# A kernel's last FFN quarter: older blocks first in the down product, two token sums in buffers of their own, a small copy from VectorE to ScalarE

## The chip, the core and the metric

The kernel runs on one core of one Trainium2 chip. The metric is the device time of one execution in microseconds (us). The engines are TensorE (PE; its weight loads are PEld), VectorE (DVE), ScalarE (ACT), GpSimd (POOL) and SyncE (SP), which issues most transfers.

## What is computed

One layer of a hybrid decoder runs over 2,064 prompt tokens (16 learned ones and 2,048) and, beside them, over 8 sampled sequences with one new token each. The mixers (an SSD scan, stick-breaking attention and a gated linear recurrence) come first; the change lies mostly in the feed-forward part behind them:

```python
h = rms_norm(x, p['norm2'])
g, u = jnp.split(jnp.einsum('bld,df->blf', h, p['w_up']), 2, axis=-1)      # 1024 -> 2 * 2816
g, ffn_buf = causal_dwconv(g, ffn_buf, p['ffn_conv_w'], p['ffn_conv_b'])   # 3 taps along the tokens
x = x + jnp.einsum('blf,fd->bld', jax.nn.silu(g) * u, p['w_down'])         # 2816 -> 1024
```

The convolution's last inputs are returned as new state, for the prompt and for each sampled sequence.

## The kernel before

All products keep float32's accuracy by splitting each operand into a rounded part and a rest (`hi`, `lo`; `wh`, `wl`) and by adding three products, so each pair of 128x128 blocks costs three matmuls.

The tokens are cut in four quarters c = 0 to 3. The last has 528 tokens and the 8 sampled ones, 536 columns, worked on as two pieces A and B of 268. The hidden width of 2,816 is 22 blocks f of 128. For the last quarter `ffn(3)` (its plan is `ffn_plan(3)`) does blocks 0 and 1 by plain products (`up`) and then five groups of four, which begin with f = 2, 6, 10, 14 and 18.

- `token_sums` (L1393 to L1409) prepares four differences t[0] to t[3] of the input's columns for each k of 0 to 3: POOL subtracts (L1406), ACT rounds to the first half `tt`, DVE takes the rest (L1409). All four results of a k lie in the ring `pg` of three buffers.
- `seven` (L1411 on) takes two blocks at once, i = 0 for the gate and i = 1 for the up part, in seven products instead of eight, with three PSUM banks. A product is 12 matmuls of 268 columns (L1423). The sums between them, on DVE (L1427), release a bank for the next product: u = banks[1] + p1 releases the bank of the product with tt[3] (called the tt30 product here), and the first use of u and banks[2] releases the one for the last product.
- `conv` adds the taps on DVE (L496, L501 for the sampled tokens), copies the prompt's state on ACT (L498) and the sampled state on DVE (L503); `gate` follows on ACT, DVE and POOL (L1387 to L1390).
- `finish` multiplies gate and up part (L1456, DVE), rounds on ACT (L168) and takes the rest on DVE (L1458): two halves of an act, of which a group needs four.
- `down` (L1488 on) multiplies a group's four acts with W_down, a quarter of the output's rows at a time: four banks of 24 matmuls (L1499), each added to the residual on DVE (L1501). A group's first down quarter is written after the gate part of the next group's first `seven`; by then two acts, the newer pair, have hardly left `finish`.

A scheduler with a simulated timeline sets the order of the instructions within each engine; the streams (main, attention, SSD, samples) are mixed by `mingle`. So an edit in one place can move instructions in others. PSUM banks are handed out in a ring of eight (`mps`).

Of the kernel before, what the change touches and what calls it, by code (L numbers as in the profile page):

```python
# [27 lines left out]
SCOL = CH + TAIL  # L28
# [11 lines left out]
def build(tc, a, o):  # L40
    nc = tc.nc
    ctx = ExitStack()
    with ctx:
# [70 lines left out]
        def pg():  # L114
            return mk(P["ph"], [128, 384], F32, "pg", N["pg"])
# [363 lines left out]
        def conv(outs, c, wts, j, hs, taps, samp, nsamp, rb=None, buf=None):  # L479

            W = ntok(c)
            nt = CH if c < 3 else CH + TAIL
            nh = taps - 1
            buf = tmp() if buf is None else buf
            acc = tmp()
            nc.scalar.copy(buf[:, 0:nh], hs[:, j, :])
            for p, c0, n in outs:
                evac(buf[:, nh + c0:nh + c0 + n], p[:, :n], None if rb is None else rb[:, c0:c0 + n])
                if rb is None:
                    nc.scalar.activation(acc[:, c0:c0 + n], p[:, :n], AF.Identity,  # L490
                                         bias=wts[:, j, taps:taps + 1], scale=wts[:, j, taps - 1:taps])
            if rb is not None:
                nc.scalar.activation(acc[:, :W], buf[:, nh:nh + W], AF.Identity,
                                     bias=wts[:, j, taps:taps + 1], scale=wts[:, j, taps - 1:taps])
            for q in range(nh):
                nc.vector.scalar_tensor_tensor(acc[:, :nt], buf[:, q:q + nt], wts[:, j, q:q + 1], acc[:, :nt],  # L496
                                               ALU.mult, ALU.add)
            nc.scalar.copy(hs[:, j, :], buf[:, nt:nt + nh])  # L498
            if c == 3:
                for q in range(nh):  # L500
                    nc.vector.scalar_tensor_tensor(acc[:, SCOL:SCOL + 8], samp[:, j, q, :], wts[:, j, q:q + 1],  # L501
                                                   acc[:, SCOL:SCOL + 8], ALU.mult, ALU.add)
                nc.vector.tensor_copy(nsamp[:, j, :], buf[:, nh + SCOL:nh + SCOL + 8])  # L503
            return acc


# [873 lines left out]
        def ffn(c):  # L1380
# [12 lines left out]
            def token_sums():  # L1393

                for n in range(4):
                    st["tt", n] = [mk(P["lp"], [128, 4, HW_], F32R, f"tt{n}{j}", 1) for j in range(2)]
                A, B = slice(0, HW_), slice(HW_, W)
                for k in range(4):
                    x = [tmp() for _ in range(2)]
                    for j in range(2):  # L1400
                        nc.scalar.activation(x[j][:, :W], xs[k + 4 * j][:, :W], AF.Copy, scale=g2[:, k + 4 * j:k + 4 * j + 1])
                    t = []
                    for n in range(4):
                        t.append(pg()[:, :HW_])
                        p, q = ((x[0][:, B], x[0][:, A]), (x[1][:, B], t[0]), (x[1][:, B], x[0][:, B]), (x[1][:, A], t[min(n, 1)]))[n]
                        nc.gpsimd.tensor_tensor(t[n], p, q, ALU.subtract)  # L1406
                        hi, lo = [z[:, k, :] for z in st["tt", n]]
                        rounded(hi, t[n])
                        nc.vector.tensor_tensor(lo, t[n], hi.bitcast(F32), ALU.subtract)  # L1409
# [78 lines left out]
            def down(g, i):  # L1488
                wh, wl = wpart()
                nd = NK // len(g)  # L1490
                for d in range(i * nd, (i + 1) * nd):
                    ds_ = slice((d - i * nd) * 128, (d - i * nd) * 128 + 128)
                    for c0, n in pieces(c):
# [302 lines left out]
```

## Time and profile before

| | us |
|---|---|
| median of 3 runs | 2878.35 (2873.82 to 2881.42) |
| the profiled execution | 2877.74 |
| its span in the trace | 2876.1 |
| PE busy in the span | 2740.2 (95%) |
| DVE, ACT, POOL busy | 1955.8, 1314.0, 1230.9 |

All steps below are worked out in the profiled execution. It lies 0.61 us under the median, and 1.6 us of it lie around the span. Times in the trace are counted from the span's start. Matmuls are pipelined, so that the durations of neighbours overlap: what a product costs is read from the start of one to the start of the next.

### The profile page before, as it was taken

What the parts mean: (1) busy time and instruction counts of PE and PEld (TensorE: products, weight loads), DVE (VectorE), ACT (ScalarE), POOL (GpSimd) and SP (SyncE); (2) the same over time, 40 slices, a digit from 0 to 9 for tenths busy, and PEclk for the clock granted to TensorE, in tenths of its full rate; (3) what the DMA queues carried; (4) which work ended last, traced back from release to release, by engine and by line L of the source; (5) the groups of instructions that cost most, each with busy time, mean ns of one, the idle gap of its engine ahead of it and who ended that gap; (6) DMA issues with size and microseconds to landing.
All of it is one profiled execution on the core that took longest, in us unless ns stands there. A gap on an engine that the chain in (4) does not pass through costs nothing. (4 is left out here: it accounts for less than half of the span.)

```text
span 2876.1 us, 44058 instructions
## 1 busy us (share of the span) xinstructions
PE 2740.2 (95%) x14901; PEld 2332.0 (81%) x14901; DVE 1955.8 (68%) x3017; ACT 1314.0 (46%) x2484; POOL 1230.9 (43%) x1597
## 2 busy tenths in 40 slices
PE   8889999899899999899998999999999999999999
PEld 6768778799878877777786788877788888989999
DVE  5673654856758689988674487777677743397775
ACT  4455766776665555445432143434333321433332
POOL 2521211312255554554655455436565530354452
PEclk9999999999999999999999999999999999999999
DMA  9878688668777865878778977675766677566665
GB/s 323 320 270 273 207 265 282 213 214 286 237 256 275 292 223 203 283 256 280 249 234 270 289 249 224 210 251 191 243 229 230 221 231 270 198 208 215 216 210 172
DMA packets 379800, 702.24 MB, mean 244 GB/s; under 512 B 69525, under 2 KB 200262, under 8 KB 379574
## 3 DMA queue, kind: packets, MB, share of 16 engines
q1 hardware_dynamic: 362758, 649.07, 67.3%
q0 software_dynamic: 16384, 50.35, 5.3%
q8 instruction: 118, 1.93, 0.3%
q14 instruction: 108, 0.88, 0.1%
q10 hardware_dynamic: 432, 0.01, 0.0%
HBM read 539.14 MB, written 160.12 MB: 243 GB/s over the span
## 5 line engine op out<-in xcount | busy, mean ns | idle before, releaser
L414 PE MATMUL mm<-hxh,w 128*128 128x512 f32 (+1 forms) x3664 | 1149.9, 387 | 35.7 <-ACT w L168 13.0
L414 PEld LDWEIGHTS mm<-hxh,w 128*128 128x128 f32 x3664 | 677.6, 191 | 173.7 <-ACT w L168 13.4
L414 PE MATMUL mm<-hxl,w 128*128 128x512 f32 (+1 forms) x1832 | 704.5, 385 | 1.2 <-DVE hxl L384 1.0
L414 PEld LDWEIGHTS mm<-hxl,w 128*128 128x128 f32 x1832 | 349.6, 191 | 66.5 <-issue 1.7
L1499 PE MATMUL mm<-ah,w 128*128 128x512 f32 (+1 forms) x968 | 329.6, 387 | 11.9 <-DVE t L1471 4.8
L496 DVE SCALAR_TENSOR_TENSOR t<-t,pack,t 128x512 f32<-128x512 f32 (+1 forms) x284 | 246.3, 867 | 60.8 <-ACT t L490 49.8
L1059 POOL COPY scy<-R 128x1 f32<-128x1 f32 (+1 forms) x245 | 107.2, 438 | 311.2 <-DVE R L1055 283.0
L1055 DVE TENSOR_TENSOR_SCAN R<-R,scy,zcol 128x512 f32<-128x512 f32 (+1 forms) x148 | 204.8, 1385 | 28.6 <-ACT R L1046 28.1
L1499 PEld LDWEIGHTS mm<-ah,w 128*128 128x128 f32 x968 | 182.6, 191 | 49.1 <-DVE x L1501 7.7
L326 POOL TENSOR_TENSOR w<-w,w 128x1024 fp32r<-128x1024 f32 x74 | 185.6, 2508 | 63.3 <-PE mm L414 22.2
L1499 PE MATMUL mm<-al,w 128*128 128x512 f32 (+1 forms) x484 | 185.6, 384 | 2.5 <-DVE al L1473 1.4
L1291 POOL TENSOR_TENSOR pg<-pg,pu 128x384 f32<-128x384 f32 x128 | 137.4, 1082 | 115.1 <-DMA pg<-in_ck 106.9
L1057 DVE TENSOR_TENSOR sz<-sz,R 128x512 f32<-128x512 f32 (+3 forms) x245 | 179.1, 732 | 3.4
L1501 DVE TENSOR_TENSOR x<-x,mm 128x512 f32<-128x512 f32 (+1 forms) x220 | 137.9, 634 | 34.1 <-PE mm L1499 33.7
L1045 ACT ACTIVATE sz<-z,pack 128x512 f32<-128x512 f32 (+3 forms) x180 | 112.2, 623 | 100.5 <-PE z L1128 87.4
L1323 POOL TENSOR_TENSOR pg<-pg,sall 128x384 f32<-128x384 f32 x120 | 115.0, 965 | 97.2 <-DMA pg<-in_cv 96.5
L1292 DVE TENSOR_REDUCE sall<-pg 128x6 f32<-128x384 f32 x128 | 69.8, 547 | 111.1 <-POOL pg L1291 104.0
L1325 DVE TENSOR_TENSOR pu<-pu,pg 128x384 f32<-128x384 f32 x120 | 80.9, 675 | 79.2 <-POOL pg L1323 71.0
L1055 DVE TENSOR_TENSOR_SCAN R<-R,zcol 128x128 f32<-128x128 f32 (+4 forms) x97 | 97.1, 1002 | 49.0 <-POOL R L1134 48.2
L1387 ACT ACTIVATE t<-t 128x512 f32<-128x512 f32 (+1 forms) x88 | 56.2, 639 | 153.8 <-DVE t L496 94.3
L1128 PE MATMUL z<-lk,lq 128*128 128x512 f32 (+3 forms) x360 | 113.0, 387 | 5.2 <-ACT R L1046 5.1
L431 PE MATMUL mm<-w,hxh 128*128 128x390 f32 (+3 forms) x432 | 115.1, 347 | 0.3 <-DMA w<-wsw_v 0.3
(2044 smaller groups left out, 6089.4 us busy)
## 6 DMA issues: line engine op xcount, KB each, us to landing
w<-wsw_up SPq DMA_DIRECT2D x184, 512.0 KB
w<-wsw_down SPq DMA_DIRECT2D x240, 256.0 KB
w<-wsw_inT SPq DMA_DIRECT2D x102, 512.0 KB
wsw_up<-w SPq DMA_DIRECT2D x88, 512.0 KB
w<-wsw_up SPq DMA_DIRECT2D x120, 256.0 KB
w<-wsw_out SPq DMA_DIRECT2D x48, 512.0 KB
pg<-in_ck POOLq DMA_DIRECT2D x128, 192.0 KB, 4.8
pg<-in_cv POOLq DMA_DIRECT2D x128, 192.0 KB, 4.6
```

Source lines behind the costliest of these rows:

```text
L326: (nc.gpsimd if far else nc.vector).tensor_tensor(lo[:, :n], raw[:, :n], hi[:, :n].bitcast(F32), ALU.subtract)
L414: st["pe"] = nc.tensor.matmul(p[:, :n], w_[:, k, :], h_[:, k, c0:c0 + n], start=(i == 0), stop=(i == 3 * NK - 1))
L431: nc.tensor.matmul(pt[i][:r, :n], h_[:, kk, :], w_[:, k, :], start=(kk == 0 and j == 0), stop=(kk == NK - 1 and j == 2))
L496: nc.vector.scalar_tensor_tensor(acc[:, :nt], buf[:, q:q + nt], wts[:, j, q:q + 1], acc[:, :nt], ALU.mult, ALU.add)
L1045: nc.scalar.activation(sz[:rr, :nk], ps[:rr, :nk], AF.Sigmoid, bias=bias)
L1055: nc.vector.tensor_tensor_scan(R[:rr, 0:nk][:, ::-1], R[:rr, 0:nk][:, ::-1], zcol[:rr].to_broadcast([rr, nk]), init, ALU.mult, ALU.add)
L1057: nc.vector.tensor_tensor(sz[:rr, :nk], sz[:rr, :nk], R[:rr, 1:nk + 1], ALU.mult)
L1128: nc.tensor.matmul(p[:, :nk], q[:, t * 128:(t + 1) * 128], kT[:, :nk], start=n == 0, stop=n == 1)
L1291: nc.gpsimd.tensor_tensor(kp, kp, qb[:, :384], ALU.mult)
L1323: nc.gpsimd.tensor_tensor(out.rearrange("p (h d) -> p h d", h=H), vp.rearrange("p (h d) -> p h d", h=H), w6, ALU.mult)
L1499: nc.tensor.matmul(p[:, :n], w_[:, x, ds_], x_[:, s_], start=(x == 0 and j == 0), stop=(x == len(g) - 1 and j == 2))
L1501: nc.vector.tensor_tensor(xs[d][:, s_], xs[d][:, s_], p[:, :n], ALU.add)
```

## The change

There are three edits.

1. In `conv`, the copy of the sampled state goes from DVE to ACT. It runs for the last quarter alone: 22 times for the FFN, 7 for the SSD part, twice for the recurrence.
2. In `token_sums`, t[2] and t[3] of each k share a tile of the pool `a5` (two buffers), and only t[0] and t[1] stay in the ring `pg`.
3. In `down`, the last quarter's first call in each group takes four banks and multiplies the two older acts into all of them (24 matmuls), and then the newer two (24). The residual's four additions follow.

```diff
--- before.py
+++ after.py
@@ -500,7 +500,7 @@
                 for q in range(nh):
                     nc.vector.scalar_tensor_tensor(acc[:, SCOL:SCOL + 8], samp[:, j, q, :], wts[:, j, q:q + 1],
                                                    acc[:, SCOL:SCOL + 8], ALU.mult, ALU.add)
-                nc.vector.tensor_copy(nsamp[:, j, :], buf[:, nh + SCOL:nh + SCOL + 8])
+                nc.scalar.copy(nsamp[:, j, :], buf[:, nh + SCOL:nh + SCOL + 8])
             return acc
 
 
@@ -1400,8 +1400,9 @@
                     for j in range(2):
                         nc.scalar.activation(x[j][:, :W], xs[k + 4 * j][:, :W], AF.Copy, scale=g2[:, k + 4 * j:k + 4 * j + 1])
                     t = []
+                    t23 = mk(P["lp"], [128, WL], F32R, "a5", 2).bitcast(F32)
                     for n in range(4):
-                        t.append(pg()[:, :HW_])
+                        t.append(pg()[:, :HW_] if n < 2 else t23[:, (n - 2) * HW_:(n - 1) * HW_])
                         p, q = ((x[0][:, B], x[0][:, A]), (x[1][:, B], t[0]), (x[1][:, B], x[0][:, B]), (x[1][:, A], t[min(n, 1)]))[n]
                         nc.gpsimd.tensor_tensor(t[n], p, q, ALU.subtract)
                         hi, lo = [z[:, k, :] for z in st["tt", n]]
@@ -1488,6 +1489,20 @@
             def down(g, i):
                 wh, wl = wpart()
                 nd = NK // len(g)
+                if c == 3 and i == 0 and len(g) == 4:
+
+                    cells = [(d, c0, n, mps()) for d in range(nd) for c0, n in pieces(c)]
+                    for xx in ((0, 1), (2, 3)):
+                        for d, c0, n, p in cells:
+                            for x in xx:
+                                hi, lo = acts[g[x]]
+                                for j, (w_, x_) in enumerate(((wh, hi), (wh, lo), (wl, hi))):
+                                    nc.tensor.matmul(p[:, :n], w_[:, x, d * 128:d * 128 + 128], x_[:, c0:c0 + n], start=(x == 0 and j == 0),
+                                                     stop=(x == 3 and j == 2))
+                    for d, c0, n, p in cells:
+                        nc.vector.tensor_tensor(xs[d][:, c0:c0 + n], xs[d][:, c0:c0 + n], p[:, :n], ALU.add)
+                    yield 0.65 * len(g) * nd
+                    return
                 for d in range(i * nd, (i + 1) * nd):
                     ds_ = slice((d - i * nd) * 128, (d - i * nd) * 128 + 128)
                     for c0, n in pieces(c):
```

The scheduler's order moves with it. On PE, in the first down quarter of the group that begins with f = 2, ahead of the tt30 product (ah, al and the first xk pair are the older acts, a5_5418 and a5_5419 the two halves of a newer one; mm, tr, mp and acc are banks). Before:

```order
L1499 MATMUL tr_5452_28484<-a5_5418_28288,w_5437_28377 128x268
L1499 MATMUL mp_5453_28498<-ah_5368_27986,w_5437_28377 128x268
L1499 MATMUL mp_5453_28498<-al_5369_27987,w_5437_28377 128x268
L1499 MATMUL mp_5453_28498<-ah_5368_27986,w_5438_28378 128x268
L1499 MATMUL mp_5453_28498<-xk_5370_27991,w_5437_28377 128x268
L1499 MATMUL mm_5451_28470<-a5_5419_28289,w_5437_28377 128x268
L1499 MATMUL mm_5451_28470<-a5_5418_28288,w_5438_28378 128x268
L1499 MATMUL tr_5452_28484<-a5_5419_28289,w_5437_28377 128x268
L1499 MATMUL tr_5452_28484<-a5_5418_28288,w_5438_28378 128x268
L1499 MATMUL mp_5453_28498<-xk_5371_27992,w_5437_28377 128x268
L1499 MATMUL mp_5453_28498<-xk_5370_27991,w_5438_28378 128x268
L1423 MATMUL mm_5425_28301<-tt30_5251_27217,w_5434_28344 128x268
```

In the changed kernel:

```order
L1500 MATMUL mp_5449_28468<-al_5365_27983,w_5433_28373 128x268
L1500 MATMUL mp_5449_28468<-ah_5364_27982,w_5434_28374 128x268
L1500 MATMUL mp_5449_28468<-xk_5366_27987,w_5433_28373 128x268
L1500 MATMUL mp_5449_28468<-xk_5367_27988,w_5433_28373 128x268
L1500 MATMUL mp_5449_28468<-xk_5366_27987,w_5434_28374 128x268
L1500 MATMUL acc_5450_28469<-ah_5364_27982,w_5433_28373 128x268
L1500 MATMUL acc_5450_28469<-al_5365_27983,w_5433_28373 128x268
L1500 MATMUL acc_5450_28469<-ah_5364_27982,w_5434_28374 128x268
L1500 MATMUL acc_5450_28469<-xk_5366_27987,w_5433_28373 128x268
L1500 MATMUL acc_5450_28469<-xk_5367_27988,w_5433_28373 128x268
L1500 MATMUL acc_5450_28469<-xk_5366_27987,w_5434_28374 128x268
L1424 MATMUL mm_5421_28297<-tt30_5251_27217,w_5430_28340 128x268
```

Ahead of the tt30 product PE now has 24 matmuls with older acts in four banks, where it had 24 in three banks, six of them with the newer act.

On POOL, at the end of the token sums (L1406 before, L1407 in the changed kernel; L301 works on weights, L1390 on the gate). Before:

```order
L1406 TENSOR_TENSOR pg_5270_27275<-t_5266_27260,pg_5268_27267 128x268
L1406 TENSOR_TENSOR pg_5273_27283<-t_5271_27279 128x268
L1406 TENSOR_TENSOR pg_5274_27287<-t_5272_27280,pg_5273_27283 128x268
L301 TENSOR_TENSOR pu_5320_27656<-raw_5284_27369,pu_5308_27565 128x512
L1406 TENSOR_TENSOR pg_5275_27291<-t_5272_27280,t_5271_27279 128x268
L1390 TENSOR_TENSOR t_5282_27354<-t_5282_27354,rb_5240_27198 128x536
L301 TENSOR_TENSOR pu_5352_27859<-raw_5287_27374 128x512
L1406 TENSOR_TENSOR pg_5276_27295<-t_5272_27280,pg_5274_27287 128x268
```

In the changed kernel:

```order
L1407 TENSOR_TENSOR a5_5265_27261<-t_5264_27258,pg_5267_27266 128x268
L1407 TENSOR_TENSOR pg_5271_27281<-t_5268_27276 128x268
L1407 TENSOR_TENSOR a5_5270_27280<-t_5269_27277,t_5268_27276 128x268
L1407 TENSOR_TENSOR pg_5272_27285<-t_5269_27277,pg_5271_27281 128x268
L1407 TENSOR_TENSOR a5_5270_27280<-t_5269_27277,pg_5272_27285 128x268
L301 TENSOR_TENSOR pu_5316_27652<-raw_5280_27365,pu_5304_27561 128x512
L301 TENSOR_TENSOR pu_5348_27855<-raw_5283_27370 128x512
L1390 TENSOR_TENSOR t_5278_27350<-t_5278_27350,rb_5240_27198 128x536
```

The last sum stood behind three operations of other kinds and the one before it behind one; now all sixteen come first.

On DVE, from the last rests of the token sums to the addition that releases the bank acc (L1471 before, L1472 in the changed kernel). Before:

```order
L1409 TENSOR_TENSOR tt31_5252_27218<-pg_5270_27275,tt30_5251_27217 128x268
L1388 TENSOR_TENSOR t_5282_27354<-t_5282_27354,t_5283_27365 128x536
L503 COPY s_ffn_conv1_5244_27209<-t_5295_27486 128x8
L1409 TENSOR_TENSOR tt01_5246_27212<-pg_5273_27283,tt00_5245_27211 128x268
L496 SCALAR_TENSOR_TENSOR t_5296_27487<-t_5295_27486,pack_71_181,t_5296_27487 128x528
L501 SCALAR_TENSOR_TENSOR t_5296_27487<-s_ffn_conv0_5243_27208,pack_71_181,t_5296_27487 128x8
L1409 TENSOR_TENSOR tt11_5248_27214<-pg_5274_27287,tt10_5247_27213 128x268
L496 SCALAR_TENSOR_TENSOR t_5296_27487<-t_5295_27486,pack_71_181,t_5296_27487 128x528
L501 SCALAR_TENSOR_TENSOR t_5296_27487<-s_ffn_conv0_5243_27208,pack_71_181,t_5296_27487 128x8
L1409 TENSOR_TENSOR tt21_5250_27216<-pg_5275_27291,tt20_5249_27215 128x268
L1471 TENSOR_TENSOR t_5282_27354<-t_5282_27354,acc_5289_27380 128x268
L1471 TENSOR_TENSOR t_5282_27354<-t_5282_27354,mm_5290_27405 128x268
```

In the changed kernel:

```order
L1410 TENSOR_TENSOR tt11_5248_27214<-pg_5272_27285,tt10_5247_27213 128x268
L313 TENSOR_TENSOR w_5308_27583<-pu_5303_27559,w_5308_27583 128x512
L1410 TENSOR_TENSOR tt31_5252_27218<-a5_5270_27280,tt30_5251_27217 128x268
L342 TENSOR_TENSOR t_5291_27482<-z_5289_27432,rb_5240_27198 128x268
L342 TENSOR_TENSOR t_5291_27482<-mm_5290_27457,rb_5240_27198 128x268
L1388 TENSOR_TENSOR t_5278_27350<-t_5278_27350,t_5279_27361 128x536
L496 SCALAR_TENSOR_TENSOR t_5292_27483<-t_5291_27482,pack_71_181,t_5292_27483 128x528
L501 SCALAR_TENSOR_TENSOR t_5292_27483<-s_ffn_conv0_5243_27208,pack_71_181,t_5292_27483 128x8
L496 SCALAR_TENSOR_TENSOR t_5292_27483<-t_5291_27482,pack_71_181,t_5292_27483 128x528
L501 SCALAR_TENSOR_TENSOR t_5292_27483<-s_ffn_conv0_5243_27208,pack_71_181,t_5292_27483 128x8
L313 TENSOR_TENSOR w_5312_27617<-pu_5311_27615,w_5312_27617 128x512
L1472 TENSOR_TENSOR t_5278_27350<-t_5278_27350,acc_5285_27376 128x268
```

The rests of the sums now end ahead of the conv of the second block, the copy of the sampled state is gone, and acc's release follows the conv.

Elsewhere, the order also differs from about 690 to 1190 us (the last quarter's input projection, attention and SSD, and the FFN of the first quarter); there ACT has nine of the copies and, over the whole kernel, 114 table loads in place of 112. The rest keeps its order.

## Rows read from the trace of the kernel before

**Rows 1.** The profile page of the whole execution: busy time, share of the span and instructions of each engine.
```profile
PE 2740.2 (95%) x14901; PEld 2332.0 (81%) x14901; DVE 1955.8 (68%) x3017; ACT 1314.0 (46%) x2484; POOL 1230.9 (43%) x1597
```

**Rows 2.** PE's waits from 2480 us to the end, which is the FFN of the last quarter: what PE waited with, on what, microseconds in total, times, longest.
```profile
PE mp L1423 <- DVE tt L1409: 4.0, 1, 4.0
PE mm L1499 <- ACT ah L168: 2.3, 2, 1.2
PE mm L1499 <- ACT a L168: 1.6, 1, 1.6
PE acc L1423 <- DVE t L1471: 1.2, 1, 1.2
PE mm L1499 <- ACT xk L168: 1.2, 1, 1.2
PE mm L1499 <- DVE al L1458: 1.1, 2, 0.5
```

**Rows 3.** PE's timeline where the token sums are first used (start, duration, engine, line, operation, how many; in brackets the pause ahead and what ended it).
```profile
2512.80 1.40 PE L1423 MATMUL mp<-tt,w 128*128 128x268 f32 x10
2518.24 0.82 PE L1423 MATMUL mp<-tt,w 128*128 128x268 f32 x2 [4.03 <-DVE tt L1409]
2520.24 3.05 PE L1423 MATMUL acc<-tt,w 128*128 128x268 f32 x12 [1.19 <-DVE t L1471]
...
2525.37 0.28 PE L1499 MATMUL mm<-ah,w 128*128 128x268 f32 x1
```

**Rows 4.** POOL's timeline at the last of the sixteen token sums of L1406, with two of the operations ahead of it.
```profile
2514.55 1.58 POOL L1390 TENSOR_TENSOR t<-t,rb 128x536 f32<-128x536 f32 x1
2516.09 1.72 POOL L301 TENSOR_TENSOR pu<-raw 128x512 f32<-128x512 f32 x1
2517.77 1.02 POOL L1406 TENSOR_TENSOR pg<-t,pg 128x268 f32<-128x268 f32 x1
```

**Rows 5.** DVE's timeline in the same place; from the first of these rows to the last it is never idle.
```profile
2503.11 0.42 DVE L342 TENSOR_TENSOR t<-tr,rb 128x268 f32<-128x268 f32 x1
...
2513.89 0.72 DVE L503 COPY s_ffn_conv<-t 128x8 f32<-128x8 f32 x1
...
2519.76 0.42 DVE L1471 TENSOR_TENSOR t<-t,acc 128x268 f32<-128x268 f32 x1
```

**Rows 6.** Busy time of each engine (with its instructions) in four stretches, then the granted clock of PE as a share of full speed, and the DMA engines' share and rate.
```profile
736.00:811.00 75.00, 65.50 (x392) 58.78 (x393) 54.60 (x106) 54.73 (x109) 22.77 (x33) 0.84 0.78 242
...
2518.00:2525.00 7.00, 5.58 (x23) 5.26 (x24) 7.00 (x11) 2.49 (x6) 4.19 (x3) 0.51 0.26 95
2654.60:2658.20 3.60, 3.60 (x17) 3.60 (x18) 2.00 (x4) 0.64 (x1) 1.05 (x1) 0.53 0.81 287
2791.00:2794.80 3.80, 3.78 (x18) 3.78 (x19) 2.09 (x4) 0.64 (x1) 1.15 (x1) 0.55 0.69 264
```

**Rows 7.** PE's timeline in the first down quarter of the groups that begin with block 2 (first four rows) and with block 6 (last three): the first matmul of the quarter, for the first group the one behind the longer pause, the tt30 product (x12), and the first matmul of the product behind it.
```profile
2582.16 0.29 PE L1499 MATMUL mm<-ah,w 128*128 128x268 f32 x1
...
2585.24 0.39 PE L1499 MATMUL mm<-a,w 128*128 128x268 f32 x1 [1.56 <-ACT a L168]
...
2587.77 1.66 PE L1423 MATMUL mm<-tt,w 128*128 128x268 f32 x12
2589.26 0.34 PE L1423 MATMUL sd<-hxh,w 128*128 128x268 f32 x1
...
2650.19 0.29 PE L1499 MATMUL mm<-ah,w 128*128 128x268 f32 x1
...
2655.99 2.55 PE L1423 MATMUL mp<-tt,w 128*128 128x268 f32 x12
2658.38 0.29 PE L1423 MATMUL acc<-hxh,w 128*128 128x268 f32 x1
```

**Rows 8.** DVE's timeline in the same two places: the second half of a newer act, the sum that releases the tt30 product's bank, and the one that releases the bank of the product behind it.
```profile
2585.22 1.64 DVE L1458 TENSOR_TENSOR a<-t,a 128x536 fp32r<-128x536 f32 x1
2586.79 0.42 DVE L1427 TENSOR_TENSOR pg<-mm,p 128x268 f32<-128x268 f32 x1
...
2588.73 0.43 DVE L1427 TENSOR_TENSOR t<-sd,pg 128x268 f32<-128x268 f32 x1
...
2652.84 1.63 DVE L1458 TENSOR_TENSOR xk<-t,xk 128x536 fp32r<-128x536 f32 x1
2654.39 0.42 DVE L1427 TENSOR_TENSOR pg<-mp,p 128x268 f32<-128x268 f32 x1
...
2656.32 0.43 DVE L1427 TENSOR_TENSOR t<-acc,pg 128x268 f32<-128x268 f32 x1
```

**Rows 9.** POOL's timeline beside the first of them.
```profile
2583.97 2.32 POOL L301 TENSOR_TENSOR pu<-raw,raw 128x512 f32<-128x512 f32 x1 [2.21 <-DVE w L313]
```

**Rows 10.** The conv's copy on DVE that is moved, in the last part, and its nearest neighbour on ACT: duration in ns (min/median/max), first and last start.
```profile
L503 DVE COPY s_ffn_conv<-t x22: 158/446/1262, 2505.3 to 2843.5; 128x8 f32<-128x8 f32 x22
...
L498 ACT COPY fhist<-t x22: 173/178/193, 2504.9 to 2843.8; 128x2 f32<-128x2 f32 x22
```

**Rows 11.** PE's two longest waits from 690 to 1200 us, and one line's table loads on ACT over the whole execution (busy us, mean ns, idle ahead).
```profile
PE mm L414 <- ACT rb L362: 4.7, 1, 4.7
PE mm L1499 <- DVE t L1471: 3.9, 1, 3.9
...
L362 ACT ACT_TABLE_LOAD x8 | 10.3, 1283 | 0.1
```

## The prediction

> **What bounds the kernel now.** First I read the page: PE is busy for 95% of the span [rows 1], so that an edit pays only where PE waits or where its clock is down. The reader should look for the few pauses of PE in the last part, not for busy time on the engines that get lighter. The list of PE's waits from 2480 us on [rows 2] shows the longest: 4.0 us on the token sums, 1.2 on the bank acc, and 6.2 in the four rows on acts (2.3, 1.6, 1.2 and 1.1), which are a longer and a shorter pause in the first down quarters of four groups. Then the timelines say what each pause hangs on, and the windows what the clock did there. PE's granted clock was 0.51 from 2518 to 2525 us, behind the two pauses of the token sums, and 0.53 and 0.55 in stretches of 3.6 and 3.8 us behind two of the four down quarters [rows 6]: about half, that is the lower of the two levels, 1.2 GHz for 2.4.
>
> **The token sums.** PE starts the product mp<-tt at 2512.80, stops after ten matmuls for 4.03 us, ends it, stops for 1.19 us until acc is released, and gets to its next down product at 2525.37 [rows 3]. In between are 36 matmuls. Twelve at full clock take 1.49 us (2587.77 to 2589.26 [rows 7]), so 36 take 4.47, and 12.57 - 4.47 = 8.1 us are lost here: 5.2 in pauses, the rest at the lower clock. That is the most this edit can give.
> The last sum is done late because POOL has three other operations among and in front of the last two sums; two of them, 1.58 and 1.72 us, stand directly in front of the last [rows 4]. With buffers of their own all sixteen come first, and none waits for DVE to empty a buffer of the ring. I take the 4.03 us as gone: the last sum then lies some 5 us earlier or more (the two rows alone give 3.3), and its rest on DVE is no longer behind the second block's conv.
> What is late next is acc. Its release ends at 2520.18 and is the end of an unbroken row of DVE work that starts at 2503.11 [rows 5]. The change takes only two copies out of it, the longer of 0.72 us [rows 5], the other near the smallest of their kind, 0.16 [rows 10]; together 0.88. The order puts the whole conv of the second block ahead of the release still. So the release comes at 2519.3 if DVE's operations last as long as now. They last long because POOL works at the same time: the copy takes between 158 and 1262 ns [rows 10]. If each of the 27 took the shortest time that its kind takes in this trace, I estimate 10.4 us in place of 17.1 and a release at 2513.5, before PE needs it (2512.80 + 1.49 = 2514.29). POOL keeps about half of the work that it did meanwhile, its sums being over, so I take the release at 2517: PE then waits 2.7 us once for 5.2 in two pieces, a gain of 2.5, and its product behind acc starts 3.2 us earlier than 2520.24. A part of the slow stretch goes with the shorter pause, 3.4 us being lost there (7.0 us at 0.51 [rows 6]); I add 0.8. **The term is -4.0 us, with ends of -0.5 and -8.1.**
> What the rows show of the two engines: L1458 runs for 1.64 us and ends at 2586.86 [rows 8], 0.57 us after the end of POOL's 2.32 us operation at 2586.29 [rows 9]. The Trainium skill ("SBUF — State Buffer", section "Who interferes with whom") says that a DVE instruction with two SBUF inputs and a GpSimd instruction that reads SBUF exclude each other for a whole instruction. These rows agree. By that rule a removed copy hands its wait to the next addition, and the two copies are worth 2 x 0.16 = 0.32 us in place of 0.88; the term would be -3.4.
>
> **The first down quarters.** Take the group that begins with block 2. PE starts at 2582.16, pauses for 1.56 us on the newer act's first half, then once more on its second, and starts the tt30 product at 2587.77 [rows 7]. After the change 24 older matmuls come first, without a pause, and end at 2582.16 + 2 x 1.49 = 2585.14. But the tt30 product needs its bank, and the addition that releases it ends at 2587.21, because DVE does L1458 for 1.64 us ahead of it [rows 8]. DVE's order is the same there after the change. So PE stands for 2.07 us in one piece. The product takes until 2588.70, the next one's bank is released at 2589.16 [rows 8], and that product starts at about 2589.2, where it now starts at 2589.26 [rows 7]. As 24 down matmuls are left behind it before and after, the gain is 0.04 us. The pause has only changed its name, from "act" to "sum of the seven products".
> The group that begins with block 6 has the same chain: older matmuls until 2650.19 + 2.98 = 2653.17, bank at 2654.81, product until 2656.30, next bank at 2656.75 [rows 8], next product at 2656.8 against 2658.38 [rows 7]: 1.6 us. That is no wait that went, but the lower clock: the tt30 product took 2658.38 - 2655.99 = 2.39 us for 1.49. If the clock falls again after the new pause, which is longer, it is nothing. The third group is like the first and the fourth like the second; the fourth has its own slow stretch at 2791 [rows 6].
> So the ends are: all pauses gone (6.2) and both slow stretches (3.6 x 0.47 + 3.8 x 0.45 = 3.4), -9.6; slow stretches behind all four pauses where two have them now, +3.4. **I take -1.0**, a third of the two slow stretches: the pause is not shorter, and half of the old ones were followed by the lower clock.
> Four banks are held instead of three ahead of tt30; the fourth one's last reader ran before the quarter starts, so I cost that at nothing. The residual's additions come later, with nothing of PE behind them at once. The last group's down quarter has no pause in the list, so 0 there.
>
> **The copies.** ACT gets 22 copies in the last part at about 0.18 us [rows 10], 4 us in 400, where DVE and POOL are the ones awaited. ACT's idle time hides them. Without that cover they would stand ahead of the four casts that PE waits for, 4 x 0.18 = 0.7 us. I take 0.
> **The reordered stretch, 690 to 1190 us.** Nothing there is computed otherwise; the order differs, ACT gets nine copies, and over the kernel two table loads more at 1.283 us each [rows 11]. PE's longest waits there are 4.7 us on ACT (L362) and 3.9 on DVE [rows 11]. Any of them may shrink or grow. I take 0, with ends of -6 and +11 (the one worked out below as a rival).
>
> **The sum:** -4.0 - 1.0 + 0 + 0 = -5.0 us on the profiled 2877.74, that is 2872.7; the median lies 0.6 higher, so **2873.4**.
>
> **The rivals.**
> A. *The waits really go.* DVE gets to the banks' releases earlier, since it is rid of the copies, and the new order leaves no pause: -9.6 and -8.1, and 2878.35 - 17.7 = 2860.7. For it: PE has 24 matmuls of ready work in front of each wait. Against it: the release at 2587.21 hangs on L1458 and POOL's 2.32 us [rows 8, 9], not on a copy. It counts from half of that, -8.9.
> B. *Everything is only renamed.* DVE holds acc until 2519.3, and each slow stretch comes back: -0.9 and 0, so 2877.5. For it: DVE is never idle over those 17 us [rows 5]. Against it: POOL's work there is less. The rule quoted above would make this likelier, since it lets DVE gain nothing as long as POOL computes.
> C. *The reordered stretch loses, and the kernel is slower.* Place: 690 to 1190 us. One new wait of the size of L362's, 4.7 us, behind the table loads (2.6) and a third of a slow spell such as the one that follows now (0.84 over 75 us: 0.16 x 75 = 12 us lost [rows 6]; a third is 4.0): +11.3, less the 5.0 gained: +6.3, 2884.6. It decides once that stretch takes over 5 us more than its 500. For it: ACT makes the scales that PE waits for. Against it: the same disorder may as well take 4.7 us away.
>
> **How the numbers follow.** Forecast 0.42 (its own range 2868 to 2877), A 0.26, B 0.18, C 0.14. A measurement of this kernel can tell about 0.3%, 8.6 us, from no change. Faster by more: A and 0.02 of the forecast's tail, 0.28. Slower by more, above 2887: 0.08 out of C, where two waits are added or one draws a whole slow spell. Within: the rest, 0.64. The range leaves out the far third of A (below 2862) and the far part of C: 2862 to 2886.
>
> **What would show it.** Right: the 4.0 us wait on L1409's rest is gone, the wait for acc is still there and longer than 1.2 us, starting near 2514; the first down quarters have one pause of about 2 us each, named by L1427's sum (L1428 in the changed kernel) and not by an act; the distance from a quarter's first matmul to the product behind tt30 is 7.1 us in the first and third group, as before, and 6.6 in the others, or 8.2 with the clock down. Wrong: no such pause in the quarters, a conv row on DVE that is much shorter beside POOL, or a start of the last part that moved by more than 3 us against before, which is the reordered stretch's doing.

## The result, and the profile after

| | before | changed |
|---|---|---|
| median of 6 runs each, us | 2881.11 (2873.82 to 2888.11) | 2862.81 (2858.39 to 2870.11) |
| ratio, 95% interval | | 0.994 (0.9925 to 0.9955) |
| the profiled execution, us | 2877.74 | 2870.11 |
| mean granted clock in it | 0.980 | 0.984 |

So the kernel is faster by 13 to 22 us in this set, and the forecast was 5. Two later sets of runs of the same kernel, on other chips, gave 0.9965 (0.995 to 0.998) and 0.9949 (0.9935 to 0.9964). The profiled execution is the slowest of the changed kernel's first six, and that of the kernel before is a quick one (2877.74 us, where 81 later executions have a mean of 2882.8), so that the two traces differ by 7.6 us only; the other two traces of the changed kernel (runs f1_after and i1_after below) serve as a check. The page:

```profile
span 2868.5 us, 44057 instructions
...
PE 2735.2 (95%) x14901; PEld 2327.2 (81%) x14901; DVE 1945.4 (68%) x2986; ACT 1318.6 (46%) x2517; POOL 1233.4 (43%) x1597
```

PE's waits from 2480 us on, in the list that answers to [rows 2]:

```profile
PE acc L1424 <- DVE t L1472: 4.1, 1, 4.1
PE mm L1424 <- DVE pg L1428: 3.1, 2, 1.8
PE mp L1424 <- DVE pg L1428: 2.4, 2, 1.2
PE acc L1424 <- DVE t L1428: 0.6, 2, 0.3
PE sd L1424 <- DVE t L1428: 0.3, 1, 0.3
```

All rows on acts are gone, and so is the one on L1409. In their place stand the sums of the seven products (L1428, 6.4 us in seven pauses) and one wait for acc of 4.1 us.

**The token sums.** PE's timeline, as in [rows 3]:

```profile
2509.96 1.65 PE L1424 MATMUL mp<-tt,w 128*128 128x268 f32 x12
2515.72 3.02 PE L1424 MATMUL acc<-tt,w 128*128 128x268 f32 x12 [4.12 <-DVE t L1472]
...
2521.22 0.43 PE L1514 MATMUL mm<-ah,w 128*128 128x268 f32 x1
```

From the product's start to the next down product it is now 11.26 us, where it was 12.57. The product runs through; the pause ahead of acc went from 1.19 to 4.12 us, and the acc product (3.02 us) still runs at the lower clock. POOL (compare [rows 4]) and then DVE (compare [rows 5]) show why:

```profile
2504.05 0.85 POOL L1407 TENSOR_TENSOR a<-t,pg 128x268 f32<-128x268 f32 x1
2508.89 1.45 POOL L301 TENSOR_TENSOR pu<-raw,pu 128x512 f32<-128x512 f32 x1 [4.00 <-DVE w L313]
2510.42 1.63 POOL L301 TENSOR_TENSOR pu<-raw 128x512 f32<-128x512 f32 x1
2512.02 1.77 POOL L1390 TENSOR_TENSOR t<-t,rb 128x536 f32<-128x536 f32 x1
```

```profile
2509.92 0.99 DVE L1388 TENSOR_TENSOR t<-t,t 128x536 f32<-128x536 f32 x1
2510.84 1.78 DVE L496 SCALAR_TENSOR_TENSOR t<-t,pack,t 128x528 f32<-128x528 f32 x1
2512.55 1.27 DVE L501 SCALAR_TENSOR_TENSOR t<-s_ffn_conv,pack,t 128x8 f32<-128x8 f32 x1
2513.74 0.76 DVE L496 SCALAR_TENSOR_TENSOR t<-t,pack,t 128x528 f32<-128x528 f32 x1
2514.42 0.21 DVE L501 SCALAR_TENSOR_TENSOR t<-s_ffn_conv,pack,t 128x8 f32<-128x8 f32 x1
...
2515.16 0.42 DVE L1472 TENSOR_TENSOR t<-t,acc 128x268 f32<-128x268 f32 x1
```

The sixteenth sum is done at 2504.90, 5.1 us ahead of the product's start, where it was 6.0 us behind it. But three operations of POOL follow that start at 2508.89, and beside them DVE's conv takes 1.78 and 1.27 us (the same two operations take 0.76 and 0.21 us directly behind, with POOL idle from 2513.79 on), so that acc's release still ends at 2515.58, 4.1 us after PE was ready.

**The first down quarters.** PE at the tt30 product and at the product behind it, for the groups that begin with block 2 and, in the second fence, with block 6 (as in [rows 7]), and then DVE beside the second (as in [rows 8]):

```profile
2582.22 2.41 PE L1424 MATMUL mm<-tt,w 128*128 128x268 f32 x12 [1.84 <-DVE pg L1428]
2584.42 0.43 PE L1424 MATMUL sd<-hxh,w 128*128 128x268 f32 x1
```

```profile
2650.46 1.76 PE L1424 MATMUL mp<-tt,w 128*128 128x268 f32 x12 [1.19 <-DVE pg L1428]
2652.49 0.36 PE L1424 MATMUL acc<-hxh,w 128*128 128x268 f32 x1 [0.27 <-DVE t L1428]
```

```profile
2648.43 1.63 DVE L1459 TENSOR_TENSOR xk<-t,xk 128x536 fp32r<-128x536 f32 x1
2649.99 0.42 DVE L1428 TENSOR_TENSOR pg<-mp,p 128x268 f32<-128x268 f32 x1
...
2651.92 0.43 DVE L1428 TENSOR_TENSOR t<-acc,pg 128x268 f32<-128x268 f32 x1
```

The pause has the name that was forecast, DVE's sum behind L1459 (1.63 us). In the first group it is 1.84 us and the clock falls (granted 0.69 over the product, which takes 2.20 us from its start to the next one's, and 0.61 from 2584.4 to 2587.0); in the second it is 1.19 us and the clock holds (granted 1.00).

**The reordered stretch.** The windows view between the same two matmuls of both kernels (the 3,601st and the 4,201st of PE, the 5,401st and the 6,001st, and the 3,601st and the 6,601st), before:

```profile
724.80:846.10 121.30, 107.62 (x603) 93.63 (x602) 74.21 (x143) 71.10 (x136) 47.13 (x50) 0.90 0.78 253
1087.00:1228.20 141.20, 127.69 (x602) 100.17 (x601) 128.28 (x152) 65.84 (x115) 70.00 (x77) 0.95 0.72 249
724.80:1350.70 625.90, 593.45 (x3002) 487.83 (x3000) 490.59 (x686) 340.38 (x612) 320.37 (x339) 0.97 0.74 254
```

and after:

```profile
724.50:835.00 110.50, 101.84 (x602) 89.26 (x601) 79.89 (x141) 71.72 (x143) 47.07 (x51) 0.95 0.82 271
1085.20:1218.70 133.50, 123.41 (x601) 97.71 (x600) 114.10 (x150) 65.79 (x111) 76.33 (x76) 0.99 0.75 261
724.50:1342.80 618.30, 587.22 (x3003) 481.39 (x3001) 486.59 (x681) 343.93 (x619) 324.09 (x339) 0.99 0.74 257
```

The first of these stretches is 10.8 us shorter and the second 7.7, both at a higher granted clock; in the rest of the stretch 11 us are lost again, and the whole is 7.6 us shorter (625.9 to 618.3). Of these 7.6 us only 1.4 are idle time of PE (32.45 to 31.08 us); 6.2 are its busy time (593.45 to 587.22 us) for the same matmuls, that is a higher clock. The order differs up to 1253 us, somewhat further than the 1190 given ahead of the prediction, and for some twenty matmuls near 2000 us.

### The profile page after: what moved, and what is told of

Its sections match the earlier page's. It is cut to its first block, busy times and chain, and to the rows that moved or that the text cites. A ratio compares the mean times of both kernels' runs of the same rounds, so it can differ in the third digit from the quotient of the medians.

```text
span 2868.5 us, 44057 instructions
## 1 busy us (share of the span) xinstructions
PE 2735.2 (95%) x14901; PEld 2327.2 (81%) x14901; DVE 1945.4 (68%) x2986; ACT 1318.6 (46%) x2517; POOL 1233.4 (43%) x1597
## 5 line engine op out<-in xcount | busy, mean ns | idle before, releaser
L1514 PE MATMUL mm<-ah,w 128*128 128x512 f32 (+1 forms) x930 | 318.5, 389 | 9.8 <-DVE x L1516 9.7
L1055 DVE TENSOR_TENSOR_SCAN R<-R,scy,zcol 128x512 f32<-128x512 f32 (+1 forms) x148 | 211.0, 1427 | 31.9 <-ACT R L1046 31.5
L1514 PEld LDWEIGHTS mm<-ah,w 128*128 128x128 f32 x930 | 174.1, 190 | 47.0 <-DVE x L1516 14.7
L1514 PE MATMUL mm<-al,w 128*128 128x512 f32 (+1 forms) x465 | 178.6, 385 | 7.0 <-DVE al L1474 7.0
L1387 ACT ACTIVATE t<-t 128x512 f32<-128x512 f32 (+1 forms) x88 | 56.2, 638 | 154.3 <-DVE t L496 96.5
```

Of the source, the lines that this page charges most:

```text
L1055: nc.vector.tensor_tensor_scan(R[:rr, 0:nk][:, ::-1], R[:rr, 0:nk][:, ::-1], zcol[:rr].to_broadcast([rr, nk]), init, ALU.mult, ALU.add)
L1514: nc.tensor.matmul(p[:, :n], w_[:, x, ds_], x_[:, s_], start=(x == 0 and j == 0), stop=(x == len(g) - 1 and j == 2))
```

## The experiments

Each kernel is timed against the kernel before on the same chip. The table has five columns, the last four from one profiled execution of each kernel: T from the first matmul of the last token-sum product ahead of acc to the 36th behind it; Q the four first down quarters, each from its first matmul to the first of the product behind tt30 (36 matmuls, 4.46 us each if nothing waits), added up; M the reordered stretch (3,601st to 6,601st matmul); L the last part (12,001st to 14,901st).

| kernel | ratio to before (95%) | T | Q | M | L |
|---|---|---|---|---|---|
| before | | 12.57 | 30.15 | 625.8 | 381.4 |
| changed, first | 0.9940 (0.9925 to 0.9955) | 11.26 | 26.20 | 618.1 | 376.7 |
| f1_after | 0.9965 (0.9950 to 0.9980) | 10.31 | 25.99 | 618.5 | 374.5 |
| i1_after | 0.9949 (0.9935 to 0.9964) | 11.25 | 26.06 | 616.5 | 376.4 |
| e1_copies | 0.9977 (0.9964 to 0.9989) | 12.77 | 27.40 | 618.6 | 379.0 |
| e2_sums | 0.9986 (0.9973 to 0.9999) | 11.20 | 30.02 | 625.7 | 379.5 |
| e3_down | 0.9991 (0.9979 to 1.0003) | 11.79 | 27.36 | 627.8 | 379.6 |
| e4_ffncopies | 0.9984 (0.9970 to 0.9999) | 11.06 | 26.28 | 624.7 | 376.0 |
| e6_mixercopies | 0.9991 (0.9981 to 1.0001) | 12.97 | 30.10 | 617.7 | 381.9 |
| f2_noffncopies | 0.9973 (0.9957 to 0.9989) | 10.63 | 27.10 | 617.7 | 376.1 |
| g2_queue | 0.9955 (0.9938 to 0.9972) | 10.32 | 18.97 | 619.3 | 372.2 |
| h1_evac | 0.9945 (0.9929 to 0.9961) | 7.44 | 26.04 | 618.2 | 372.5 |
| h2_both | 0.9934 (0.9914 to 0.9954) | 8.05 | 18.13 | 616.6 | 370.8 |
| j1_all | 0.9930 (0.9916 to 0.9944) | 8.66 | 18.13 | 616.5 | 367.4 |

### Where the gain is: the parts alone

Theory: half of it lies in the reordered stretch, at which the prediction set 0. Rival: the last part does it all.

**e4_ffncopies**, the changed kernel with the mixers' nine copies left on DVE:

```diff
-nc.scalar.copy(nsamp[:, j, :], ...)
+(nc.scalar.copy if rb is not None else nc.vector.tensor_copy)(nsamp[:, j, :], ...)
```

> All three edits, but the nine copies of the mixers' convs stay on DVE, so that the last part has the changed kernel's order and the stretch from 690 to 1190 us has the order of before. Two theories of where the median's 18 us came from. Theory 1 (reordered stretch): the last part gives about 5 us, as in the two profiled executions (from 2490 us on), and the rest came from the reordered stretch: 4 to 7 us faster than before, ratio 0.9975 to 0.9985. Theory 2 (the last part does it, by lower-clock spells that its pauses no longer draw): 14 to 18 us faster, ratio 0.994 to 0.995.

**e6_mixercopies**, the kernel before with only those nine moved:

```diff
-nc.vector.tensor_copy(nsamp[:, j, :], ...)
+(nc.vector.tensor_copy if rb is not None else nc.scalar.copy)(nsamp[:, j, :], ...)
```

> The kernel before with only the nine copies of the mixers' convs on ACT: the stretch from 690 to 1190 us has the changed kernel's order, the last part the order of before. Theory 1 (reordered stretch): 8 to 12 us faster than before, ratio 0.996 to 0.997, and the start of the last quarter's FFN (first token sum) lies some 8 us earlier in the trace. Theory 2 (last part): within 3 us, ratio 0.999 to 1.001.

e4 has the short last part (376.0) and the old M (624.7), e6 the new M (617.7) and the old last part (381.9). So the traces split cleanly: the ten with the new order of the stretch have 616.5 to 619.3 us there, the four with the old one 624.7 to 627.8: **8.2 us** between their means, and that order comes from the nine copies alone. The last part gives 5.5 (381.4 to 375.9, the mean of the three traces of the changed kernel). Together that is 13.7 us, or a ratio of 0.9952, in the middle of the three measured. These two stretches are not the whole trace. What lies outside of them is 4.8 to 10.6 us longer in the three traces of the changed kernel (1873.7 to 1879.5 us) than in the one of the kernel before (1868.9), so that the spans differ by 3.7 to 8.5 us only. In the other traces with the old order it is up to 1877.0 us, in those with the new one down to 1871.7: much of it is spread between executions, and whether the new order also loses 2 or 3 us there can't be told. The rival falls: e4 is at 0.9984, not at 0.995. The timings of the parts are less clean than the traces: e6 at 0.9991 is a gain of 2.6 us, and the end of its interval, 5.5, does not reach 8.2. e1, with the same order in the stretch, is at 0.9977. In its profiled execution e6 lost 5.3 us ahead of the stretch (730.1 us to the 3,601st matmul, 724.8 in the kernel before), 3.0 of them in a longer wait for a transfer (3.3 us for 0.3); but that execution is the quickest of its twelve, and what the others lost is left open.

**e2_sums** (the change's second edit alone), **e3_down** (its third alone) and **e1_copies** (its first alone):

```diff
 e1  -nc.vector.tensor_copy(nsamp ...)    +nc.scalar.copy(nsamp ...)
 e2  +t23 = mk(...)
     -t.append(pg()[:, :HW_])             +t.append(pg()[:, :HW_] if n < 2 else t23[...])
 e3  +if c == 3 and i == 0 and len(g) == 4: (the new branch of down)
```

> The kernel before with the second edit alone (two token sums in buffers of their own). My prediction's step: the 4.0 us wait goes, the wait for acc stays at 2 to 4 us, -4 us in all, ratio 0.9985. From the two profiled executions: -1.2 to -1.7 us, ratio 0.9995, since DVE is held by POOL ahead of acc's release as before. Theory 2: up to -8 us, ratio 0.997.

> The kernel before with the third edit alone (two older acts first into four banks). My prediction's step: the pause moves to the sum on DVE that releases the tt30 product's bank, -1 us (0 to -3), ratio 0.999 to 1.000. Theory 1 agrees with up to -3 us, the steps seen between the two profiled executions. Theory 2: -8 to -10 us, pauses and lower-clock spells gone, ratio 0.9965 to 0.997.

> The kernel before with the first edit alone (all 31 copies on ACT). Theory 1: the reordered stretch gives what e6_mixercopies gave, 2 to 4 us, and the FFN copies nothing: ratio 0.9985 to 0.9995. Theory 2: the copies are what the rest needs: 0.996 or less.

In the last part e2, e3 and e1 give 1.9, 1.8 and 2.4 us, 6.1 together: the parts add up there, and none needs the others (L differs by up to 2.2 us between traces of the changed kernel, so that each of these gains is rough). Their timings add up too: 0.9986, 0.9991 and 0.9977 make 0.9954, some 13 us. e1's ratio lies between its two theories, and e2's interval can't tell the forecast of 4 us from the 1.2 to 1.7 read in the traces. e2 has its gain in T (11.20), e3 in Q (27.36). e1, too, has a shorter Q (27.40): with the copies off DVE the pauses on the newer act are shorter (0.8 us for 1.2 in three groups). And M is short in e1 (618.6), old in e2 and e3.

**f2_noffncopies**, the changed kernel with the 22 FFN copies back on DVE (the mirror image of e4's edit):

> The changed kernel with the 22 FFN copies back on DVE (the mixers' nine stay on ACT): both orders as in the changed kernel but for those copies. My prediction costs these copies at nothing, but for 0.3 to 0.9 us ahead of acc's release: as the changed kernel, within 0.0005 of its ratio. Rival: DVE, rid of them, is what lets the pauses shrink: slower than the changed kernel by 3 us or more (0.001).

Within the interval nothing can be told from the changed kernel (0.9973 beside 0.9965 on the same chip), but Q can: three of the quarters take 6.71 to 6.73 us where the changed kernel has 6.34. **0.37 us in each of three groups is what the FFN copies are worth**. DVE ahead of the pause in the second group, in f2_noffncopies:

```profile
2632.76 0.17 DVE L503 COPY s_ffn_conv<-t 128x8 f32<-128x8 f32 x1 [1.03 <-POOL t L1528]
2632.93 0.69 DVE L313 TENSOR_TENSOR w<-pu,w 128x512 fp32r<-128x512 f32 x1
```

and in i1_after, the changed kernel:

```profile
2639.35 0.69 DVE L313 TENSOR_TENSOR w<-pu,w 128x512 fp32r<-128x512 f32 x1 [0.90 <-ACT w L168]
```

The copy takes 0.17 us, but it stands in DVE's queue until POOL is done with its input. L313 behind it starts 10.33 us ahead of the down quarter's first matmul (2643.26), where the changed kernel starts it 10.71 us ahead (2650.06), and the row of DVE work from there to the release has no gap to make up for it.

**f1_after**, the changed kernel unaltered:

> The changed kernel once more, unaltered. The parts measured alone gave ratios of 0.9984 (last part), 0.9991 (reordered stretch); together 0.9975, 7 us. Theory 1 (the parts add up, and the first measurement of six runs drew few lower-clock spells): 0.9965 to 0.998. Theory 2 (the edits help one another, the sum is more than the parts): 0.993 to 0.9955 again, with a granted clock of 0.985 or more in most runs where the kernel before has 0.980.

0.9965 is at the edge of theory 1, but the first measurement and i1_after lie in the range of theory 2. Its sign, a clock of 0.985 or more in most runs, is met in five of the twelve. The traces speak for theory 1: in M and L the changed kernel's three have what the parts' traces have, 13.7 us in sum, and nothing beyond it; and the three edits measured one by one give 0.9954 together, as much as the whole. It is mainly the timing of e6 that falls short of its trace, 2.6 us for 8.2; e4's 4.6 us is near the 5.4 of its last part.

### What PE waits for in the last part

**g2_queue** takes away what makes DVE late: its queue is turned round. The newer act's second half and the second newer act's multiplication are issued behind the two sums. (Left out here: `finish` puts these steps of the newer acts on the list `late`.)

```diff
-add(out[1][:, B], banks[2], u)
+ib = add(out[1][:, B], banks[2], u)
+if late:
+    with tc.issue_after(ib.ins):
+        while late:
+            late.pop(0)()
 ...
-for xx in ((0, 1), (2, 3)):
+for xx in ((0, 1), (2,), (3,)):
```

> The changed kernel with DVE's queue turned round at the four first down quarters: the sum that releases the tt30 product's bank and the one that releases the next product's bank stand ahead of the newer act's second half and of the other newer act's multiplication (before, behind them). The two newer acts are multiplied one after the other, each into all four banks. Nothing else moves. My theory (PE waits for that sum, and the sum only for its place in DVE's queue behind an operation that POOL holds up): the pauses of 1.2 to 1.8 us and of 0.3 us ahead of the tt30 product and the product behind it fall to under 0.2 us; PE may wait up to 0.5 us for a newer act in their place; the four quarters together give 4 to 6 us, with the lower-clock spell behind the first gone up to 7. Rival (the newer acts are the limit anyway, whatever stands ahead): the pauses come back in front of the newer acts with 1.2 us or more, and the gain is under 1 us.

Q falls from 26.06 to 18.97, with 17.8 as the least: the theory on the wait is right, and the newer acts were not the limit. But L falls by 4.2 us only (376.4 to 372.2), and the time does not change measurably (0.9955 beside 0.9949 on the same chip). PE's waits from 2480 us on:

```profile
PE acc L1424 <- DVE t L1487: 4.1, 1, 4.1
PE mm L1424 <- ACT p L1432: 4.0, 4, 1.3
PE mp L1424 <- DVE pg L1428: 0.6, 1, 0.6
```

There is a new wait of up to 1.3 us in each of the four groups, on the copy of the first product's bank (p). ACT's timeline at the first:

```profile
2599.31 0.61 ACT L168 CAST w<-pu 128x512 fp32r<-128x512 f32 x1
2602.91 0.65 ACT L1387 ACTIVATE t<-t 128x536 f32<-128x536 f32 x1 [2.99 <-DVE t L501]
2603.47 0.17 ACT L486 COPY t<-fhist 128x2 f32<-128x2 f32 x1
2603.55 0.38 ACT L1432 COPY p<-mm 128x268 f32<-128x268 f32 x1
```

The copy stands behind a sigmoid (L1387) that waits 2.99 us for DVE's conv; PE reaches the product that needs the bank 1.2 us too early. The pause went to the next stop.

**j1_all** has the edits of g2_queue and of h1_evac (below) and puts that copy ahead of the sigmoid (left out here: the gate of the second block goes on the list `gates`):

```diff
-nc.scalar.copy(p1, banks[0])
+cp1 = nc.scalar.copy(p1, banks[0])
+if gates:
+    with tc.issue_after(cp1.ins):
+        while gates:
+            gates.pop(0)()
 ...
```

> The kernel with both edits (g2_queue's and h1_evac's), and on ACT the copy of the first product's bank (p1) now stands ahead of the second block's sigmoid in each group's second seven products, where it was behind. Theory: the 1.2 us wait per group that g2_queue and h2_both show on that copy, four times, was the pause of the first down quarters at its next stop, for p1 was ready but queued behind a sigmoid that waits for DVE: it falls to under 0.3 us each, and the last part is 4 to 5 us shorter than h2_both's in the trace. Ratio to the kernel before 0.991 to 0.9935. Rival (POOL's and DVE's chain of the conv sets the pace): the pause comes back at the next act or sum with about the same length, and under 1.5 us are gained on h2_both in the trace.

```profile
PE tr L1424 <- ACT p L1432: 2.8, 1, 2.8
PE tr L1424 <- DVE pg L1428: 0.7, 2, 0.3
PE z L1424 <- DVE pg L1428: 0.5, 2, 0.3
```

The four waits on that copy are gone (0.3 us each are left on DVE's sum), and L falls from h2_both's 370.8 to 367.4, by 3.4 and not by 4 to 5. One spell at the lower clock came back in that execution (granted 0.50 from 2512.3 to 2515.7 us), which h2_both's does not have in the last part; T, where it lies, is 0.6 us longer. The rival said under 1.5.

**h1_evac** lets ACT empty acc as soon as the product is done (the changed kernel for the rest):

```diff
+uo = mk(P["lp"], [128, WL], F32, "uc", 2) if c == 3 else None
 for p, c0, n in ou:
+    if c == 3:
+        nc.scalar.copy(uo[:, c0:c0 + n], p[:, :n])
+for p, c0, n in ou if c < 3 else ((uo, 0, W),):
     s_ = slice(c0, c0 + n)
     nc.vector.tensor_tensor(g[:, s_], g[:, s_], p[:, :n], ALU.mult)
```

> The changed kernel, but ACT copies the up product's banks of blocks 0 and 1 to a buffer as soon as they are done, and DVE multiplies the gate from there later; so the bank acc is released by ACT and not by DVE's addition-like product behind POOL's work. My theory (the 4.1 us wait for acc is a wait for DVE's place in the gate chain, the bank itself being read late): that wait goes to under 1 us, with 4 to 6 us gained in the trace (the spell at the lower clock behind it may go as well). Rival (PE is then held by the next thing in the chain, the acts of blocks 0 and 1 for the first down product): the wait moves behind the acc product, and under 2 us are gained.

PE's waits from 2480 to 2580 us:

```profile
PE tr L1424 <- ACT p L1432: 2.7, 1, 2.7
PE mm L1518 <- ACT ah L168: 0.9, 1, 0.9
```

The wait for acc is gone. Of its 4.1 us, 2.7 come back one product later on ACT's copy p and 0.9 on the acts of blocks 0 and 1, as the rival had it. Yet L is 3.9 us shorter than i1_after's, just under the theory's 4 to 6 and more than the rival's 2: the lower clock is gone from the last part in this execution, and the gain is that alone. PE is idle there for 10.6 us in i1_after and 10.7 in h1_evac, and busy for 365.8 and 361.8. The timing (0.9945 beside 0.9949) can't tell it from nothing.

**h2_both** has g2_queue's and h1_evac's edits, and **i1_after** is the changed kernel on the same chip:

> Both of the edits of the two kernels beside this one, on top of the changed kernel. If they act in different places, as theory has it, their gains add up: 8 to 11 us less than the changed kernel, ratio to the kernel before 0.992 to 0.994. If PE's time is set by something else in the last part, no more than 3 us less than the changed kernel.

> The changed kernel once more, on the same chip as the three variants, so that they can be compared with it: ratio to the kernel before 0.9965 again, or between 0.994 and 0.998, as the two measurements so far.

h2_both is 5.6 us shorter than i1_after in L; the ratios, 0.9934 and 0.9949, differ by 4.3 us and their intervals overlap. That is more than the 3 us of the rival and less than the 8 to 11 of the sum that was expected: part of what the two edits free comes back on the copy p (4.8 us in four waits, and 2.7 in one). j1_all's (0.9930, 0.9916 to 0.9944) is the lowest of all and clear of the kernel before; against the changed kernel (0.9949 and 0.9965 in the later sets) it may be some 5 to 10 us faster, but it ran on another chip, and its interval overlaps two of that kernel's three (all but f1_after's).

## Why the prediction was right and wrong

- **The last part, forecast -5.0: measured -5.5** (three traces). The sum came out by luck: one of its two terms was too large by about as much as the other was too small. The whole, forecast -5 and measured -10 to -18 by the medians of the three sets, is short by the reordered stretch below; the first median, 2862.81, lies at the very end of the range of 2862 to 2886.
- **The token sums, forecast -4.0: measured -1.3 to -2.3** (T 12.57 to 11.26, 10.31 and 11.25). The wait of 4.03 us went as said, and acc was late next as said. The failing size is "I take the release at 2517: PE then waits 2.7 us": it waits 4.1. I took POOL as half idle there, and so it is (4.9 us of work between 2504.9 and 2515.4). But its three operations run just beside DVE's conv ahead of acc and hold it, 1.78 and 1.27 us for 0.76 and 0.21. Rival B was nearer.
- **The first quarters, forecast -1.0: measured -4.0** (Q 30.15 to about 26.1). The mechanism was right to the name: the older products run through, the pause is DVE's sum, and g2_queue, which takes away that queue's order, takes away the pause. Two sizes were off. The first is the clock: "half of the old ones were followed by the lower clock", and I counted a third of the two slow stretches as gained. Two of the four quarters take 8.2 to 8.6 us in each of before, e2_sums and e6_mixercopies, one at most is slowed at all in each of the changed kernel's three traces and in e3_down (7.0 to 7.2 us in the first group, the others 6.3 to 6.7). That gives about 3 us, of which e3_down has 2.8. Why pauses of the same length draw the lower clock in the old order and seldom in the new one is open. The second is the copies: "I take 0" counts them on ACT; on DVE they hold up the queue and are worth 0.37 us in each of three groups.
- **The reordered stretch: "I take 0, with ends of -6 and +11" failed: -8.2 us**, outside the ends, and the largest part of the gain. I named L362's wait of 4.7 us [rows 11] and did not follow it in the order of ACT, which was known. ACT before, where PE waits until 736.55, and the row of DVE that it hangs on:

```profile
730.33 0.70 ACT L1046 ACTIVATE R<-z,sbn 128x512 f32<-128x512 f32 x1
734.08 0.52 ACT L400 ACTIVATE su<-su 128x384 bf16<-128x384 f32 x1 [3.05 <-DVE su L962]
734.51 0.19 ACT L400 ACTIVATION_READ_ACCUMULATOR su<-su 128x1 f32 x1
734.72 1.28 ACT L362 ACT_TABLE_LOAD   x1
736.01 0.86 ACT L362 ACTIVATE rb<-mm,eps 128x268 f32<-128x268 f32 x2
...
733.49 0.56 DVE L962 TENSOR_TENSOR su<-su,su 128x384 f32<-128x384 f32 x1 [2.14 <-DMA su<-z]
```

and in the changed kernel, where PE waits 0.70 us until 732.60:

```profile
730.05 0.70 ACT L1046 ACTIVATE R<-z,sbn 128x512 f32<-128x512 f32 x1
730.77 1.28 ACT L362 ACT_TABLE_LOAD   x1
732.07 0.86 ACT L362 ACTIVATE rb<-mm,eps 128x268 f32<-128x268 f32 x2
732.82 0.52 ACT L400 ACTIVATE su<-su 128x384 bf16<-128x384 f32 x1
```

Before, the table load and the scale (L362) stood behind L400, which waits 3.05 us for DVE and through it for a transfer; now they come first, and PE's wait is 0.7 us in all ten traces with the new order. This wait is only a part of the 8.2 us. In the other traces with the old order it is 2.0 (e2), 4.3 (e3) and 2.5 us (e4), since DVE waits for the transfer 0.2 and 1.8 us and not at all there, and M is 625.7, 627.8 and 624.7 all the same. The larger part is the clock, as the busy time above says: the granted clock is 0.95 for 0.90 in the first of the two stretches and 0.99 for 0.95 in the second, 360 us later. Which of the moved pauses account for that was not followed. So this was no chance of the runs, as the fourteen traces show, though it is no purpose of the edit either: nine tiny copies moved the order that the scheduler made.
- **Rival A's time (2860.7) came out, but not its mechanism:** its waits did not go. Rival C was the right place with the wrong sign.
- The signs listed under "what would show it" were met in the main: one pause of 1.1 to 1.9 us in each quarter, named by L1428, and a wait on acc longer than 1.2 us. The distances of 7.1 us in the first and third group and 6.6 in the others came out as 7.0 to 7.2 in the first and 6.3 to 6.4 in the other three; the third group was not like the first before either (6.67 and 7.10 us). The sign that was to give the reordered stretch away did not: the start of the last part moved by 2.8 us only in the first trace, since the stretch behind, whose order is nearly unchanged, took 5.1 us longer in that execution.

## What to carry to other kernels

Where a scheduler orders the work, an edit's side effects on that order can outweigh the edit: follow each long wait of PE through the orders of both kernels, engine by engine, before setting a stretch at zero. Ask of every pause not only what ends it but what stands ahead of that on its engine; when the queue is turned round, ask the same of the next stop. A tiny operation is not free by its size: it holds its engine's queue until its own input is there.

## What the runs showed of the hardware

Executions of one kernel differed by 5 to 21 us here, in good part with the granted clock: over the runs of the kernel before in four of these comparisons (81) the mean time is 2882.8 us at a mean clock of 0.980, over the changed kernel's 24 runs 2869.5 at 0.985. The difference of 13.3 us is close to the 13.7 of the two stretches. In the trace of the kernel before a pause of 1.15 us was followed by a spell at the lower level (granted 0.53) in the second of the four quarters, and one of 1.17 us in the third was not (8.20 and 6.67 us). So a single profiled execution can be off by some us in any stretch.
